# Row copies on two engines, second-head buffers and reordered tasks in a one-core hybrid decoder layer

## The chip, the cores and the metric

The kernel runs on one core of a Trainium2 chip. The metric is device time in microseconds (us) of one execution. The engines are named as in the profile: PE (TensorE, matrix multiply), PEld (its weight loads), DVE (VectorE), ACT (ScalarE), POOL (GpSimd) and SP (SyncE, which issues most of the DMAs). Each engine works through its own queue in order.

## The reference

One decoder layer for 256 tokens behind 16 learned meta tokens (272 rows in all), width 4096, in f32. A first projection (4096 to 16384 columns) gives eight kinds of columns, and two branches of 16 heads (or channel groups) of 128 use them:

```
h = rmsnorm(x, norm_g)
q, k, v, g_attn, b_conv, c_conv, h_conv, z_conv = split(h @ w_in)      # 8 x 2048 columns
# stick-breaking attention, per head, keys s before query t only
A[t, s] = sigmoid(z_ts) * prod_{s<j<t} (1 - sigmoid(z_tj)),  z = q.k / sqrt(128)
o = group_rmsnorm((A @ v) * silu(g_attn), attn_norm_g, 16)
# short gated convolution, width 3, per channel
y = group_rmsnorm(b_conv * short_conv(c_conv * h_conv, conv_w) * silu(z_conv), conv_norm_g, 16)
out = rmsnorm(x + concat(o, y) @ w_out, final_norm_g)[16:]
```

## The kernel before, in words

**Splits.** Every f32 weight tile (128x1024, 512 KB) is split into a rounded part `wh` (a copy on ACT, line 399) and a rest `wl` (a subtraction on DVE, line 395). The activations are split once in the same way. Each product is then three fp32r matmuls: high by low, high by high, low by high. A tile pair of `wh` and `wl` lives in a ring of six (`RING`), so the split of a tile waits until PE has finished the sixth one before it.

**Pieces.** The whole kernel is a list of 880 pieces, numbered 0 to 879, that PE works through in order. The input projection has eight groups; group g makes the columns of heads 2g and 2g+1 (in the code u = 0 and u = 1) and of the two channel groups beside them. A group has two kinds of pieces. A block piece `p` (24 matmuls, lines 424 to 426) does eight 128-row steps of one head's k, v, c or h block, transposed (128 features by 272 or 258 positions). The row pieces make q, g, b and z by rows: a plain pair A, B has 12 matmuls of 512 columns in each piece (lines 432 to 435), and a pair treated as two-by-two blocks with seven products has four pieces A, B, T, U of 6, 3, 6 and 6 matmuls, for which DVE forms the sums T and U (lines 409 to 414).

**Zones.** A group begins with its R zone: four times two block pieces (the last c and h blocks of the group before) and a plain pair. Then follows its S zone: twelve times A, B, T, U and two block pieces (the first six blocks of the group itself). After the last group a Z zone follows, and then the output projection as groups 8 to 11 of row pieces, with eight thin pieces `o` at the end. Where the text below names piece numbers, 417 to 432 is the R zone of group 5, in which the attention of group 4 is done, and 433 begins its S zone.

**What sets the order.** The order of every queue is written out by hand. At step i the program issues the matmuls of piece i, then the split of the piece five further on (line 985 to 987), then what the end of a block needs, and then the tasks that are due at i. `later(at, fn)` puts a task on the list; a `yield k` in it means: go on k pieces later. `plan_group` gives the due pieces of a group's attention, counted from its last S piece (`fin[g]`, here 416). For each of the two heads there are four tasks:

- `scores`: two matmuls z on PE; one piece later zm on DVE (lines 738 and 740) and Abs, Tanh and Ln on ACT (743 to 745)
- `weights`: four operations on DVE with two scans (751 to 755); one piece later four Exp on ACT (761 to 764)
- `trans`: a DVE transpose (770) within 32x32 blocks; one piece later `blocks`, 16 small copies on ACT (562) that move the blocks to their places, and two smaller ones on DVE (774, 775)
- `po`: ten matmul instructions on PE (779 to 783) that multiply the weights with v, and one piece later a product on DVE (787)

Between Tanh, Ln and Exp the ACT engine loads function tables, which the profile shows as instructions of their own. `v_block` has a task of the same shape: a transpose (579), then 16 copies (562) and four (585) on ACT.

**Buffers.** In the pool `wk` a tile with a tag waits for the last use of the tile that had the tag before. The scores of both heads use the tags zm and zl. Of the eight PSUM banks the R zone leaves three to the tasks, and the S zone one, which is also the bank of its block pieces. So the transposes `mix_t` of the group before (`mxh` and `mxc`, line 702), six and eight quads into an S zone, need that DVE has read the block that ended just before them (`c_block`, line 592, reads the block of c).

**Group sums of the output.** For groups 0 to 6 the normalised branch outputs go to DRAM and come back by the pieces `m`, whose split (lines 371 and 372) is followed by sums on POOL (305 to 308) for the seven-product pairs. `out_sums` (line 869) empties four PSUM banks after the last U piece of an output group. `load_res` (858) loads residual and gain, on SP's queue, into tiles of which one has the tag cb1 of the last group's rows.

Of the kernel before, what the change touches and what calls it, by code (L numbers as in the profile page):

```python
# [8 lines left out]
F32 = mybir.dt.float32  # L9
# [101 lines left out]
def kernel(ctx, tc, xt, xin, xm, par, fg, w1, w2, out):  # L111
# [48 lines left out]
    for g in range(GROUPS, GROUPS + 4):  # L160
        for at_, j in enumerate(OUT_ORDER if g > GROUPS else OUT_FIRST):
            for q in "ABTU" if seven(g, j) else "AB":
                pieces.append((q, g, j))
                if g == GROUPS and (at_, q) in ((2, "A"), (3, "A"), (9, "A")):
                    pieces.append(ms[{2: 4, 3: 5, 9: 6}[at_]])
        fin[g] = len(pieces) - 1
# [3 lines left out]
    real = [i for i, p in enumerate(pieces) if p[0] in "ABTUpo"]  # L170
    nth = {i: q for q, i in enumerate(real)}

# [380 lines left out]

    def blocks(dst, src, n):

        d = dst.rearrange("p (c x) -> p c x", c=n)
        s = src.rearrange("p (c x) -> p c x", c=n)
        for i in range(4):
            for j in range(4):
                o = d[32 * j:32 * j + 32, :, 32 * i:32 * i + 32]  # L560
                x = s[32 * i:32 * i + 32, :, 32 * j:32 * j + 32]
                A.copy(out=o, in_=x)  # L562

# [8 lines left out]
    def v_block(u, src, at_):  # L572
        vt = wk.tile([P, L + META], F32, tag="vt", name=f"vt{u}")
        G.memset(vt[:, L:L + META], 0.0)
        V.tensor_tensor(out=vt[:, :L], in0=src, in1=rstd, op=ALU.mult)

        def vtrans():
            y = wk.tile([P, 416], F32, tag="zs", name=f"yv{u}")
            V.transpose(out=y[:, :L + META], in_=vt[:, :L + META])
            yield 1  # L580
            vv = wk.tile([P, 2 * P], F32, tag=f"vv{u % 2}", name=f"vv{u}")
            blocks(vv, y[:, :2 * P], 2)
            v3 = wk.tile([META, P], F32, tag=f"v3{u % 2}", name=f"v3{u}")
            for i in range(4):
                A.copy(out=v3[:, 32 * i:32 * i + 32], in_=y[32 * i:32 * i + META, 2 * P:2 * P + 32])
            hd[u, "v"] = (vv, v3)

        later(at_, vtrans)
# [21 lines left out]
    def plain_block(u, b, e):  # L610
# [3 lines left out]
        elif b == 1:  # L614
            v_block(u, ps[:, :L], after(e, 2 if u % 2 == 0 else 3))
        elif b == 2:
            c_block(u, ps[:, META - 2:L])
        else:
            h_block(u, ps[:, META - 2:L], after(e, 1))
# [110 lines left out]
    def scores(g, u):  # L730
# [5 lines left out]
        yield 1  # L736
        zm = wk.tile([P, 448], F32, tag="zm", name=f"zm{g}_{u}")[:, :ZW]
        V.scalar_tensor_tensor(out=zm[:, :144], in0=z[:, :144], scalar=rq[:, 0:1], in1=zmask[:, P:],
                               op0=ALU.mult, op1=ALU.add)
        V.scalar_tensor_tensor(out=zm[:, 144:], in0=z[:, 144:ZW], scalar=rq[:, 1:2], in1=zmask,  # L740
                               op0=ALU.mult, op1=ALU.add)
        l = wk.tile([P, 448], F32, tag="zl", name=f"zl{g}_{u}")[:, :ZW]
        A.activation(out=l, in_=zm, func=AF.Abs)
# [4 lines left out]
    def weights(g, u):  # L748
# [8 lines left out]

        za = wk.tile([P, 448], F32, tag="zm", name=f"za{g}_{u}")
        G.memset(za[:, 3 * P:], 0.0)
# [7 lines left out]
    def trans(g, u):  # L767
        za = gr[g].pop(("za", u))
        y = wk.tile([P, 448], F32, tag="zl", name=f"ya{g}_{u}")
        V.transpose(out=y, in_=za)  # L770
        yield 1
        blocks(at[:, P:], y[:, :3 * P], 3)

# [45 lines left out]
    def plan_group(g):  # L819
# [4 lines left out]
        later(after(f, 1), q_t, g)  # L824
        for u, z in ((0, 5), (1, 10)):
            later(after(f, z), scores, g, u)
            later(after(f, z + 3), weights, g, u)
            later(after(f, z + 5), trans, g, u)
            later(after(f, z + 8), po, g, u)
        e = ends[2 * g + 1, 3]  # L830
        later(after(e, 4) if end else slot(g + 1, 2), conv_t, (2 * g, 2 * g + 1))
        later(after(e, 6) if end else after(slot(g + 1, 2), 2), conv_out, g)
        later(after(f, 20), squares, g, "h")
        later(after(f, 19) if end else slot(g + 1, 4), squares, g, "c")
        later(after(f, 21) if end else after(slot(g + 1, 4), 1), norm, g)
        later(after(f, 23) if end else slot(g + 1, 6), mix, g, "h")
        later(after(f, 24) if end else slot(g + 1, 8), mix, g, "c")

# [30 lines left out]
    def out_sums(g):  # L869
# [8 lines left out]
        V.tensor_tensor(out=r12, in0=p5, in1=r12, op=ALU.add)  # L878
        V.tensor_tensor(out=r22, in0=p5, in1=r22, op=ALU.add)
        V.tensor_tensor(out=r12, in0=r12, in1=s, op=ALU.subtract)  # L880
        V.tensor_tensor(out=s, in0=p7, in1=s, op=ALU.add)  # L881
        V.tensor_tensor(out=r21, in0=r21, in1=s, op=ALU.add)
        V.tensor_tensor(out=r22, in0=r22, in1=s, op=ALU.subtract)
# [79 lines left out]
    for i in range(1 - SPLITS, n):  # L963
# [34 lines left out]
        elif p[0] in "ABTUm":  # L998
            mm_in(i)
            while halved < until:  # L1000
                split(halved)
                halved += 1
            g = p[1]
            if p[0] == "B" and p[2] in (10, 6):
                load_res(2 * (g - GROUPS) + (p[2] == (6 if g > GROUPS else 10)))
            if p[0] == "U" and p[2] == OUT_SJ[-1]:
                out_sums(g)
            if i == fin[g]:
# [96 lines left out]
```

## Time and profile before

| | |
|---|---|
| median of 3 runs | 1907.0 us (1905.54 to 1907.43) |
| profiled execution | 1903.0 us |
| its span, first to last instruction | 1901.0 us |
| mean granted TensorE clock | 0.979 |
| PE busy | 1818.4 us (96%) |
| DVE, ACT, POOL busy | 1504.2, 1204.9, 146.7 us |
| input projection with its attention | to about 1519 us |
| one group of it | about 190 us |

The profiled execution is 2 us longer than its span, and the median of the runs 4 us longer than the profiled execution. The view of waits lists for an engine and line what released it, then total, count and longest. The timeline gives start, duration, engine, line, operation, output and inputs, and in brackets the idle time just before; several like instructions in a row are merged (x4). In the table of windows the columns are busy time with counts by engine, then the granted clock of PE, the share of the DMA engines and GB/s.

### The profile page before, as it was taken

The page shows a single profiled execution, that of the slowest core. Times are in us where ns is not written, and L with a number is a line of the kernel's source. Part 1 is how long each engine was busy: PE and PEld are TensorE (multiplying, and loading weights), DVE is VectorE, ACT ScalarE, POOL GpSimd, SP SyncE. Part 2 cuts the span into 40 slices and gives each one's busy share as a digit, 9 for nine tenths or more (in the row PEclk, how much of TensorE's full clock was granted, in tenths as well). Part 3 has the DMA queues.
Part 4 walks back from the last instruction along what each step waited for, and adds up shares of the span by engine and source line. Part 5 has one row for each costly group of instructions (what it writes and reads, how often), then busy time and mean ns, then how long its engine had stood idle before and what let it go on. Part 6 is the DMA issues. An engine that isn't in the chain of part 4 may idle for free. (4 is left out here: it accounts for less than half of the span.)

```text
span 1901.0 us, 29647 instructions
## 1 busy us (share of the span) xinstructions
PE 1818.4 (96%) x10998; PEld 1633.5 (86%) x10998; DVE 1504.2 (79%) x1858; ACT 1204.9 (63%) x2012; POOL 146.7 (8%) x192
## 2 busy tenths in 40 slices
PE   9999999999999999999999999999999979999997
PEld 7899788978897989798979897989798967788897
DVE  6765789678967896789778967897689768998986
ACT  6755765676567656665666566656665775555553
POOL 2031010001000100010101000100010131000000
PEclk9999999999999999999999999999899989999999
DMA  8966457645764576457645764576457654575664
GB/s 302 323 234 215 147 190 252 212 145 192 248 214 147 194 246 211 151 192 244 211 154 192 243 211 153 193 245 213 146 192 244 221 185 163 199 239 203 229 207 181
DMA packets 116064, 393.64 MB, mean 207 GB/s; under 512 B 13008, under 2 KB 18256, under 8 KB 115920
## 3 DMA queue, kind: packets, MB, share of 16 engines
q1 hardware_dynamic: 111888, 388.08, 61.0%
q10 hardware_dynamic: 4032, 3.67, 0.6%
q8 instruction: 86, 1.41, 0.3%
q14 instruction: 58, 0.48, 0.1%
HBM read 380.17 MB, written 11.53 MB: 206 GB/s over the span
## 5 line engine op out<-in xcount | busy, mean ns | idle before, releaser
L395 DVE TENSOR_TENSOR wl<-raw,wh 128x1024 fp32r<-128x1024 f32 (+3 forms) x756 | 848.5, 1143 | 304.2 <-ACT wh L399 294.6
L399 ACT CAST wh<-raw 128x1024 fp32r<-128x1024 f32 (+3 forms) x756 | 707.8, 974 | 333.9 <-DVE raw L414 87.8
L426 PE MATMUL mm<-xs,wl 128*128 128x258 f32 (+1 forms) x2048 | 582.6, 284 | 4.8 <-DVE wl L395 4.8
L424 PE MATMUL mm<-xs,wh 128*128 128x258 f32 (+1 forms) x2048 | 585.4, 286 | 0.0
L425 PE MATMUL mm<-xs,wh 128*128 128x258 f32 (+1 forms) x2048 | 582.2, 284 | 0.0
L424 PEld LDWEIGHTS mm<-xs,wh 128*128 128x128 f32 x2048 | 386.1, 189 | 6.8 <-DVE cq L787 1.2
L426 PEld LDWEIGHTS mm<-xs,wl 128*128 128x128 f32 x2048 | 386.0, 188 | 6.2 <-DVE wl L395 6.2
L425 PEld LDWEIGHTS mm<-xs,wh 128*128 128x128 f32 x2048 | 386.1, 189 | 4.1
L432 PE MATMUL P<-wh,xs 128*128 128x512 f32 x604 | 239.1, 396 | 3.8 <-DVE cc L597 2.3
L399 ACT CAST wh<-t 128x1024 fp32r<-128x1024 f32 (+1 forms) x108 | 112.4, 1041 | 201.4 <-DVE t L409 114.1
L435 PE MATMUL P<-wl,xs 128*128 128x512 f32 x604 | 237.2, 393 | 0.5 <-DVE wl L395 0.5
L434 PE MATMUL P<-wh,xs 128*128 128x512 f32 x604 | 236.3, 391 | 0.0
L432 PE MATMUL P<-wh,mixl 128*128 128x512 f32 (+1 forms) x392 | 150.0, 383 | 1.9 <-DVE os L881 1.9
L435 PE MATMUL P<-wl,mixh 128*128 128x512 f32 (+1 forms) x392 | 149.2, 381 | 2.7 <-DVE wl L395 2.7
L434 PE MATMUL P<-wh,mixh 128*128 128x512 f32 (+1 forms) x392 | 148.8, 380 | 0.0
L395 DVE TENSOR_TENSOR wl<-t,wh 128x1024 fp32r<-128x1024 f32 (+1 forms) x108 | 131.7, 1220 | 12.2 <-ACT wh L399 12.2
L435 PEld LDWEIGHTS P<-wl,xs 128*128 128x128 f32 x604 | 114.1, 189 | 28.3 <-DVE wl L395 4.1
L432 PEld LDWEIGHTS P<-wh,xs 128*128 128x128 f32 x604 | 114.4, 189 | 26.8 <-ACT za L764 5.1
L409 DVE TENSOR_TENSOR t<-raw,raw 128x1024 f32<-128x1024 f32 (+1 forms) x108 | 131.8, 1220 | 2.3 <-DMA raw<-w 2.3
L434 PEld LDWEIGHTS P<-wh,xs 128*128 128x128 f32 x604 | 114.3, 189 | 20.0
L435 PEld LDWEIGHTS P<-wl,mixh 128*128 128x128 f32 x392 | 74.5, 190 | 16.3 <-DVE wl L395 4.4
L432 PEld LDWEIGHTS P<-wh,mixl 128*128 128x128 f32 x392 | 74.7, 191 | 14.4 <-DVE os L881 2.4
(246 smaller groups left out, 2102.7 us busy)
## 6 DMA issues: line engine op xcount, KB each, us to landing
raw<-w SPq DMA_DIRECT2D x614, 512.0 KB, 4.3
lent<-sumd SPq DMA_DIRECT2D x49, 512.0 KB, 6.1
raw<-w SPq DMA_DIRECT2D x32, 384.0 KB, 3.8
raw<-xin SPq DMA_DIRECT2D x8, 512.0 KB, 5.7
xr<-xt SPq DMA_DIRECT2D x15, 272.0 KB, 5.6
sumd<-lent SPq DMA_DIRECT2D x7, 512.0 KB, 3.0
raw<-mixd SPq DMA_DIRECT2D x7, 512.0 KB, 4.9
res<-xin SPq DMA_DIRECT2D x12, 256.0 KB, 4.7
```

The costliest lines, as they stand in the source:

```text
L395: nc.vector.tensor_tensor(out=lo[:, c], in0=t[:, c], in1=h[:, c].bitcast(F32), op=ALU.subtract)
L399: nc.scalar.copy(out=h[:, c], in_=t[:, c])
L409: nc.vector.tensor_tensor(out=s[:, :2 * hw].rearrange("p (a b) -> p a b", a=2), in0=a[:, :2 * hw].rearrange("p (a b) -> p a b", a=2), in1= ...
L424: nc.tensor.matmul(out=o, lhsT=h, rhs=x[:, 0, s:], start=k == 0, stop=False)
L425: nc.tensor.matmul(out=o, lhsT=h, rhs=x[:, 1, s:], start=False, stop=False)
L426: nc.tensor.matmul(out=o, lhsT=lo, rhs=x[:, 0, s:], start=False, stop=k == KC - 1)
L432: nc.tensor.matmul(out=o, lhsT=a[1], rhs=h, start=key not in begun, stop=False)
L434: nc.tensor.matmul(out=o, lhsT=a[0], rhs=h, start=False, stop=False)
L435: nc.tensor.matmul(out=o, lhsT=a[0], rhs=lo, start=False, stop=last)
```

## The change

It has five parts.

1. `blocks` is cut into two halves of eight copies, the second one piece after the first, and of the eight copies four run on ACT and four on DVE. This holds for the attention weights (16 units, 32x96 elements a copy) and for v (16 units, 32x64).
2. The second head's scores and weights get their own buffers: two of the tag u2 in place of zm, and kT0 in place of zl.
3. The due pieces of a group's attention change. Before, the first head had 5, 8, 10, 13 (scores, weights, trans, po) and the second 10, 13, 15, 18. Now the first has 4, 7, 10, 13 and the second 6, 9, 13, 17. In the last group squares, norm and mix come one piece earlier (in the others only `squares` of the attention branch does). The v task of the first head starts six pieces after its block and not two.
4. The `m` pieces of groups 4, 5 and 6 stand later in output group 8: behind the fifth, sixth and eighth pair in place of the second, third and ninth (counted from 0).
5. In the output groups `out_sums` is issued ahead of the split of its step, and in it the second read of the product P5 comes after the read of P7.

```diff
-                if g == GROUPS and (at_, q) in ((2, "A"), (3, "A"), (9, "A")):
-                    pieces.append(ms[{2: 4, 3: 5, 9: 6}[at_]])
+                if g == GROUPS and (at_, q) in ((5, "A"), (6, "A"), (8, "A")):
+                    pieces.append(ms[{5: 4, 6: 5, 8: 6}[at_]])
...
-    nth = {i: q for q, i in enumerate(real)}
+    nth = {i: sum(k < i for k in real) for i in range(n)}
...
-    def blocks(dst, src, n):
+    def blocks(dst, src, n, half):
...
-        for i in range(4):
+        for i in (0, 1) if half == 0 else (2, 3):
             for j in range(4):
                 o = d[32 * j:32 * j + 32, :, 32 * i:32 * i + 32]
                 x = s[32 * i:32 * i + 32, :, 32 * j:32 * j + 32]
-                A.copy(out=o, in_=x)
+                if (i + j) % 2:
+                    V.tensor_copy(out=o, in_=x)
+                else:
+                    A.copy(out=o, in_=x)
...
-            blocks(vv, y[:, :2 * P], 2)
+            blocks(vv, y[:, :2 * P], 2, 0)
+            yield 1
+            blocks(vv, y[:, :2 * P], 2, 1)
...
-            v_block(u, ps[:, :L], after(e, 2 if u % 2 == 0 else 3))
+            v_block(u, ps[:, :L], after(e, 6 if u % 2 == 0 else 3))
...
-        zm = wk.tile([P, 448], F32, tag="zm", name=f"zm{g}_{u}")[:, :ZW]
+        zm = wk.tile([P, 512], F32, tag="u2", name=f"zm{g}_{u}", bufs=2) if u else wk.tile([P, 448], F32, tag="zm", name=f"zm{g}_{u}")
+        zm = zm[:, :ZW]
...
-        l = wk.tile([P, 448], F32, tag="zl", name=f"zl{g}_{u}")[:, :ZW]
+        l = wk.tile([P, 448], F32, tag="kT0" if u else "zl", name=f"zl{g}_{u}")[:, :ZW]
...
-        blocks(at[:, P:], y[:, :3 * P], 3)
+        blocks(at[:, P:], y[:, :3 * P], 3, 0)
+        yield 1
+        blocks(at[:, P:], y[:, :3 * P], 3, 1)
...
-        for u, z in ((0, 5), (1, 10)):
-            later(after(f, z), scores, g, u)
-            later(after(f, z + 3), weights, g, u)
-            later(after(f, z + 5), trans, g, u)
-            later(after(f, z + 8), po, g, u)
+        for u, at_ in enumerate(((4, 7, 10, 13), (6, 9, 13, 17))):
+            for k, fn in zip(at_, (scores, weights, trans, po)):
+                later(after(f, k), fn, g, u)
...
-        V.tensor_tensor(out=r22, in0=p5, in1=r22, op=ALU.add)
         V.tensor_tensor(out=r12, in0=r12, in1=s, op=ALU.subtract)
         V.tensor_tensor(out=s, in0=p7, in1=s, op=ALU.add)
+        V.tensor_tensor(out=r22, in0=p5, in1=r22, op=ALU.add)
...
             mm_in(i)
+            g = p[1]
+            if p[0] == "U" and p[2] == OUT_SJ[-1]:
+                out_sums(g)
             while halved < until:
                 split(halved)
                 halved += 1
```

The first place is ACT's queue in the R zone of group 5 (pieces 417 to 432), where the attention of group 4 is done. The names zm4_0 and zm4_1 are those of the first and the second head; wh428 is the split of piece 428. Before:

```order
L399 CAST wh428_9818<-raw428_9692 128x1024
L399 CAST wh429_9836<-raw429_9732 128x1024
L399 CAST wh430_9874<-raw430_9765 128x1024
L761 ACT_TABLE_LOAD
L761 ACTIVATE za4_0_9878<-zs4_0_9840 128x256
L762 ACTIVATE za4_0_9878<-zs4_0_9840 128x128
L763 ACTIVATE za4_0_9878<-zs4_0_9840 128x16
L764 ACTIVATE za4_0_9878<-zs4_0_9840 128x16
L399 CAST wh431_9910<-raw431_9804 128x1024
L399 CAST wh432_9931<-raw432_9822 128x1024
L562 COPY at_109<-ya4_0_9914 32x3x32 x16
```

And with the change, at the same place:

```order
L399 CAST wh428_9821<-raw428_9692 128x1024
L749 ACTIVATE zl4_1_9833<-zm4_1_9830 128x416
L750 ACT_TABLE_LOAD
L750 ACTIVATE zl4_1_9833<-zl4_1_9833 128x416
L751 ACT_TABLE_LOAD
L751 ACTIVATE zl4_1_9833<-zl4_1_9833,half_120 128x416
L399 CAST wh429_9851<-raw429_9722 128x1024
L768 ACT_TABLE_LOAD
L768 ACTIVATE za4_0_9855<-zs4_0_9825 128x256
```

The second head's Abs, Tanh and Ln, which stood behind the first head's copies, now stand ahead of the first head's Exp, with a table load ahead of Tanh that was not there; the second head's Exp in turn needs no load of its own.

The second place is DVE's queue in the same zone, from the last of the first head's four operations of `weights` to its transpose. Before:

```order
L755 TENSOR_TENSOR zs4_0_9840<-zm4_0_9797,zl4_0_9800 128x416
L395 TENSOR_TENSOR wl430_9875<-raw430_9765,wh430_9874 128x1024
L395 TENSOR_TENSOR wl431_9911<-raw431_9804,wh431_9910 128x1024
L770 STREAM_TRANSPOSE ya4_0_9914<-za4_0_9878 128x448
L395 TENSOR_TENSOR wl432_9932<-raw432_9822,wh432_9931 128x1024
L774 COPY at_109<-ya4_0_9914 16x16
```

And with the change:

```order
L761 TENSOR_TENSOR zs4_0_9825<-zm4_0_9752,zl4_0_9755 128x416
L744 SCALAR_TENSOR_TENSOR zm4_1_9830<-z4_1_9804,rq_124,zmask_113 128x144
L746 SCALAR_TENSOR_TENSOR zm4_1_9830<-z4_1_9804,rq_124,zmask_113 128x272
L395 TENSOR_TENSOR wl429_9852<-raw429_9722,wh429_9851 128x1024
L395 TENSOR_TENSOR wl430_9891<-raw430_9772,wh430_9890 128x1024
L757 SCALAR_TENSOR_TENSOR zs4_1_9894<-zm4_1_9830,zl4_1_9833 128x416
L759 SCALAR_TENSOR_TENSOR zl4_1_9833<-one_118,zs4_1_9894 128x144
L759 SCALAR_TENSOR_TENSOR zl4_1_9833<-one_118,zs4_1_9894 128x272
L761 TENSOR_TENSOR zs4_1_9894<-zm4_1_9830,zl4_1_9833 128x416
L395 TENSOR_TENSOR wl431_9926<-raw431_9807,wh431_9925 128x1024
L777 STREAM_TRANSPOSE ya4_0_9929<-za4_0_9855 128x448
```

Both the second head's zm and its four operations of `weights` moved ahead of the first head's transpose.

The third place is DVE's queue at the end of output group 8, where `out_sums` empties the banks (P4_8 is the product P1, P5_8 P5, P6_8 P7 and P7_8 P6). Before:

```order
L395 TENSOR_TENSOR wl742_16583<-raw742_16541,wh742_16582 128x1024
L876 TENSOR_TENSOR res0_15754<-P4_8_16247,res0_15754 128x512
L877 TENSOR_TENSOR os8_16586<-P7_8_16304,os8_16586 128x512
L878 TENSOR_TENSOR res0_15754<-P5_8_16287,res0_15754 128x512
L879 TENSOR_TENSOR res1_15755<-P5_8_16287,res1_15755 128x512
L880 TENSOR_TENSOR res0_15754<-res0_15754,os8_16586 128x512
L881 TENSOR_TENSOR os8_16586<-P6_8_16291,os8_16586 128x512
```

And with the change:

```order
L883 TENSOR_TENSOR res0_15770<-P4_8_16263,res0_15770 128x512
L884 TENSOR_TENSOR os8_16582<-P7_8_16310,os8_16582 128x512
L885 TENSOR_TENSOR res0_15770<-P5_8_16295,res0_15770 128x512
L886 TENSOR_TENSOR res0_15770<-res0_15770,os8_16582 128x512
L887 TENSOR_TENSOR os8_16582<-P6_8_16299,os8_16582 128x512
L888 TENSOR_TENSOR res1_15771<-P5_8_16295,res1_15771 128x512
L889 TENSOR_TENSOR res1_15771<-res1_15771,os8_16582 128x512
L890 TENSOR_TENSOR res1_15771<-res1_15771,os8_16582 128x512
L395 TENSOR_TENSOR wl742_16593<-raw742_16541,wh742_16592 128x1024
```

The split wl742 moved behind the eight operations, and the read of bank P6_8 stands one operation nearer to the front of them.

More of the change, by code (lines that the diff above doesn't have):

```diff
@@ L756, in weights @@
         yield 1
-        za = wk.tile([P, 448], F32, tag="zm", name=f"za{g}_{u}")
+        za = wk.tile([P, 512], F32, tag="u2", name=f"za{g}_{u}", bufs=2) if u else wk.tile([P, 448], F32, tag="zm", name=f"za{g}_{u}")
+        za = za[:, :448]
         G.memset(za[:, 3 * P:], 0.0)
@@ L768, in trans @@
         za = gr[g].pop(("za", u))
-        y = wk.tile([P, 448], F32, tag="zl", name=f"ya{g}_{u}")
+        y = wk.tile([P, 448], F32, tag="kT0" if u else "zl", name=f"ya{g}_{u}")
         V.transpose(out=y, in_=za)
         yield 1
-        blocks(at[:, P:], y[:, :3 * P], 3)
+        blocks(at[:, P:], y[:, :3 * P], 3, 0)
+        yield 1
+        blocks(at[:, P:], y[:, :3 * P], 3, 1)
         V.tensor_copy(out=at[:META, P - META:P], in_=y[96:96 + META, 400:416])
@@ L832, in plan_group @@
         later(after(e, 6) if end else after(slot(g + 1, 2), 2), conv_out, g)
[L833 to L837, printed above, removed]
+        later(after(f, 19), squares, g, "h")
+        later(after(f, 18) if end else slot(g + 1, 4), squares, g, "c")
+        later(after(f, 20) if end else after(slot(g + 1, 4), 1), norm, g)
+        later(after(f, 22) if end else slot(g + 1, 6), mix, g, "h")
+        later(after(f, 23) if end else slot(g + 1, 8), mix, g, "c")
     res, fgs, acc, sqs = [], {}, [], []
@@ L1002 @@
                 halved += 1
-            g = p[1]
             if p[0] == "B" and p[2] in (10, 6):
                 load_res(2 * (g - GROUPS) + (p[2] == (6 if g > GROUPS else 10)))
-            if p[0] == "U" and p[2] == OUT_SJ[-1]:
-                out_sums(g)
             if i == fin[g]:
```

## The prediction

> **What bounds the kernel now.** I read the page's busy shares first, then the waits of PE, then the timeline and the table of windows at the places of those waits.
>
> ```profile
> span 1901.0 us, 29647 instructions
> PE 1818.4 (96%) x10998; PEld 1633.5 (86%) x10998; DVE 1504.2 (79%) x1858; ACT 1204.9 (63%) x2012; POOL 146.7 (8%) x192
> ...
> PE po L779 <- ACT at L562: 39.3, 9, 7.4
> PE mxh L702 <- DVE cc L592: 11.5, 7, 1.7
> PE mm L426 <- DVE wl L395: 4.8, 7, 0.7
> PE P L432 <- DVE cc L597: 2.3, 7, 0.4
> ...
> 412.10:418.90 6.80, 6.80 (x19) 5.19 (x19) 6.73 (x8) 3.66 (x9) 0.00 (x0) 0.50 0.61 213
> ...
> 1560.96 0.80 PE L779 MATMUL po<-vv,at 128*128 128x128 f32 x2 [7.40 <-ACT at L562]
> ```
>
> PE bounds the span, so only its idle time and its slow time can be won. Of 82.6 us idle, 39.3 stand before `po`: 4.2 us in each of the seven R zones that follow groups 0 to 6, always at the second head, and the rest in the last group (7.40 there). The window row shows a second price: after such a wait PE runs at half clock for about 6.8 us, which loses 3.4. So a boundary costs 4.24 + 0.32 (the last wait row, 2.3 by 7) + 3.4 = 8.0 us, and seven cost 56.
>
> **The change part by part: the seven boundaries.** The question is when the first head's 16 copies are done now, since `po` of the first head stands at the same piece as before (after 429), and the second head's chain has moved ahead of it. These are rows of group 4's boundary.
>
> ```profile
> 936.47 0.28 PE L424 MATMUL mm<-xs,wh 128*128 128x258 f32 x1
> 963.11 0.38 PE L779 MATMUL po<-vv,at 128*128 128x128 f32 x2
> 964.50 0.39 PE L424 MATMUL mm<-xs,wh 128*128 128x258 f32 x1
> ...
> 938.79 0.90 ACT L585 COPY v<-yv 16x32 f32<-16x32 f32 x4
> 944.24 0.55 ACT L743 ACTIVATE zl<-zm 128x416 f32<-128x416 f32 x1 [2.53 <-DVE zm L740]
> 945.40 1.28 ACT L745 ACT_TABLE_LOAD   x1
> 946.69 0.64 ACT L745 ACTIVATE zl<-zl,half 128x416 f32<-128x416 f32 x1
> 947.24 2.94 ACT L399 CAST wh<-raw 128x1024 fp32r<-128x1024 f32 x3
> 952.94 0.42 ACT L761 ACTIVATE za<-zs 128x256 f32<-128x256 f32 x1 [1.46 <-DVE zs L755]
> 953.68 1.98 ACT L399 CAST wh<-raw 128x1024 fp32r<-128x1024 f32 x2
> 956.55 4.49 ACT L562 COPY at<-ya 32x96 f32<-32x96 f32 x16 [0.90 <-DVE ya L770]
> ...
> 943.72 0.49 DVE L740 SCALAR_TENSOR_TENSOR zm<-z,rq,zmask 128x272 f32<-128x272 f32 x1
> 950.58 0.58 DVE L751 SCALAR_TENSOR_TENSOR zs<-zm,zl 128x416 f32<-128x416 f32 x1
> 952.82 1.22 DVE L395 TENSOR_TENSOR wl<-raw,wh 128x1024 fp32r<-128x1024 f32 x1
> 955.88 0.64 DVE L770 STREAM_TRANSPOSE ya<-za 128x448 f32<-128x448 f32 x1
> 957.75 0.16 DVE L775 COPY a<-ya 16x16 f32<-16x16 f32 x1
> ```
>
> Steps read off them: Abs, Tanh, load, Ln take ACT 3.00 (944.24 to 947.24), and 4.28 with a second load of 1.28; four Exp 0.74; the four operations of `weights` 2.24 on DVE; zm 0.77; a split 1.05 on ACT (0.95 within a run) and 1.14 on DVE; a copy 0.28 on ACT. Before 936.47 the queues are as they were. With the change, in this group:
>
> - Piece 420 ends at 936.47 and frees the ring for 426: wh426 to 937.5, wl426 to 938.7, zm of the first head to 939.5.
> - ACT: its Abs to Ln 3.00, to 942.5; the second four v copies 1.0 and the four of line 585 0.9, to 944.4; wh427 to 945.5, wh428 to 946.4. Then ACT must wait.
> - DVE: wl427 behind wh427 to 946.6, the c block 0.34, wl428 to 948.1, `weights` of the first head 2.24 to 950.35, zm of the second to 951.1.
> - ACT: Abs to Ln of the second head, two loads, 4.28, to 955.4; wh429 to 956.5; load 1.3; the first head's Exp, 957.8 to 958.5; wh430 to 959.5 and wh431.
> - DVE: wl430 to 960.7; `weights` of the second head 2.24, to 962.9; wl431 to 964.1; only then the first head's transpose, to 964.7.
> - ACT: four copies to 965.9, wh433 to 966.9, four to 967.9. DVE: wl433 behind wh433 to 968.1, four copies, the two small ones: 969.0.
>
> PE wants `po` at 963.1 as before (two z products lie ahead of it in both), so **a wait of 5.9 us appears at the first head**. The price of a DVE copy of 32x96 isn't in the trace; the nearest rows:
>
> ```profile
> L774 DVE COPY at<-ya 16x16 f32<-16x16 f32 x16 | 2.7, 167 | 0.5
> L603 DVE TENSOR_SCALAR cy<-cc,pt 128x256 f32<-128x256 f32 x16 | 5.8, 364 | 0.6
> ```
>
> By elements 96 lies between them at about 0.23 us alone, and 0.15 in a run, since the two small copies start 0.09 apart. Only the last four of them lie on this chain (0.6; at the ends of the range 0.35 and 1.45), so the wait is 5.6 to 6.8.
>
> At the second head nothing waits: its transpose is done by 972.8, and after 969.0 `po` and pieces 430 to 433 take PE to about 983; the DVE queue (sums of pair 434, the h block, the convolution of 1.7) reaches its last copy at 981.6. That is 1.5 us of cover; if it is gone, each further us costs seven. The half clock remains: `po` doubles its 1.39 (963.11 to 964.50), and a block piece loses nearly half its speed for the remaining 4 us, 3.4 in all, as before. So a boundary costs 5.9 + 3.4 = 9.3 against 8.0: **+1.3 each, +9 for seven** (bounds +7 and +16; 0 if I am out by one split).
>
> On the clock, "TensorE: Matmul & The Clock Gate" (Part 1) of the Trainium skill says that PE drops to half rate after about 3.4 us without work and needs one busy window of 3.4 to come back. The waits of 4.24 agree with the first; the 6.8 us in the window row are two windows, not one, and I use the row.
>
> On table loads, the Trainium skill, "ScalarE: Activation LUTs" (What ACT_TABLE_LOAD costs), gives 1.28 us and a drain of 1.38 for each. Here Ln starts 0.01 after its load ends (945.40 + 1.28 to 946.69), so the trace shows no drain. With it the four loads on the chain would add 5.5, and the sum would end near 1950; the sum goes by the row.
>
> **S zones.** The v task of the first head moves from the second quad's start to the end of it, and half of its copies to DVE. The rows of group 5's S zone (the norm of the group before runs there too):
>
> ```profile
> 1030.48 4.06 ACT L562 COPY vv<-yv 32x64 f32<-32x64 f32 x16
> 1038.68 1.23 DVE L395 TENSOR_TENSOR wl<-raw,wh 128x1024 fp32r<-128x1024 f32 x1 [0.89 <-ACT wh L399]
> 1040.80 3.50 DVE L395 TENSOR_TENSOR wl<-raw,wh 128x1024 fp32r<-128x1024 f32 x3 [0.90 <-ACT wh L399]
> 1044.21 1.22 DVE L409 TENSOR_TENSOR t<-raw,raw 128x1024 f32<-128x1024 f32 x1
> 1050.96 0.42 DVE L592 TENSOR_TENSOR cc<-mm,rstd 128x258 f32<-128x258 f32 x1
> 1051.53 0.63 PE L702 MATMUL mxh<-ident,cq 128*128 128x128 f32 x4 [1.64 <-DVE cc L592]
> ```
>
> Today the 16 copies and four more hold ACT for 5 us, and DVE idles 1.75, 0.89 and 0.90 behind it. From 1044.21 DVE is full until the c block frees the bank. With the change the copies come behind wh468: wl467 ends at 1040.0, the transpose at 1040.4, ACT's first four at 1041.4, wl469 at 1043.6, and four DVE copies fill the time to 1044.2. So the sums start where they did, and PE restarts at 1051.5: the wait of 0.69 goes and returns in the next, 2.3 in one piece. Sum 0 (bounds -1 and +1 each). But one wait of 2.3 us may cost clock:
>
> ```profile
> 1588.20 0.47 PE L432 MATMUL P<-wh,osum 128*128 128x512 f32 x1 [2.32 <-DVE mixl L718]
> ...
> 1589.70:1593.10 3.40, 3.40 (x10) 2.62 (x9) 2.73 (x4) 2.10 (x4) 0.00 (x0) 0.50 0.71 292
> ...
> 1635.87 0.50 PE L432 MATMUL P<-wh,mixl 128*128 128x512 f32 x1 [1.95 <-DVE os L881]
> ```
>
> After 2.32 the clock halved for 3.4 us, a loss of 1.7; the waits of 1.64 and 1.95 cost none. If four of seven are hit that is 6.8, at most 12; I take **+4**.
>
> **The last group.** Here the splits of `m` pieces take places in the lead, and the same order hurts earlier.
>
> ```profile
> 1506.75 0.43 DVE L592 TENSOR_TENSOR cc<-mm,rstd 128x258 f32<-128x258 f32 x1 [2.95 <-PE mm L426]
> ...
> 1524.66 0.59 PE L432 MATMUL P<-wh,mixl 128*128 128x512 f32 x1
> ```
>
> From the c block's end, 1507.2, by the same steps: four DVE copies, wl690, one `m` rest and zm, to 1510.9; on ACT Abs to Ln, eight copies, one `m` copy and two splits, to 1518.7; on DVE the `m` rest, two splits, `weights` and the second zm, to 1523.3; ACT 4.3 for the second head, to 1527.6, and only then wh695, to 1528.7. PE wants piece 695 at 1524.66 as today, and waits 4. Exp, the second head's `weights`, the convolution and two splits lead to the first head's transpose at 1541.0 and its last copy at 1545.2, where PE has been waiting since 1540.5: `po` of the first head comes at 1545 and not 1536, and the second at 1561 as today, without the 7.40. To there the two are about even. Then it wins: the `m` sums are out of the way, and `mxc` comes at 1579 (six pieces of 12 matmuls at 0.23, and 1.8 for `po` and `mxh`, after 1560.8), not 1583.2. What hangs on that:
>
> ```profile
> 1583.86 0.33 SPq L866 DMA_DIRECT2D fg<-fg  x1
> 1590.30 1.22 DVE L409 TENSOR_TENSOR t<-raw,raw 128x1024 f32<-128x1024 f32 x1 [2.25 <-DMA raw<-w]
> ...
> 1866.75 0.39 PE L901 MATMUL mo<-keep,mixl 128*128 128x256 f32 x1 [1.88 <-DVE res L876]
> ```
>
> SP's queue stands at the gain's load, whose tile `mxc` has to leave, and the next weights wait behind it until 1590.30; from there to `out_sums` DVE has no gap. The DVE queue then starts about 4.2 us earlier and has two sums (1.2) less to do, and `out_sums` stands ahead of one split (1.2) with one operation (0.6) less before the bank that PE wants: together 7.2 us, of which PE can take nearly all: **-7** (bounds -12 and 0). At the end the 1.88 before `mo` go, since `out_sums` no longer stands behind splits that wait for weights: **-1.9**.
>
> **Sum.** 9 + 4 - 7 - 2 = +4 on 1903.0, the profiled execution (its span plus 2), so 1907; the median of the runs lies 4 above it, at 1907.0, and becomes **1911**.
>
> **The rivals.**
>
> - The clock doesn't care for 2.3 us. By the rule of the clock page of the Trainium skill named above, only windows without work count. The 1.95 without loss speaks for it, the 2.32 with loss against it. Then the +4 go: 1907, no change. Chance 0.27.
> - The boundaries are won: the first head's copies come by 963 and the second's too. All 56 us and 9 at the tail would go: 1842. If they come 4 us before my 969.0 the wait stays under 2, keeps the clock and wins 6 each: about 1860. It needs wl430 and `weights` of the second head not to stand ahead of the first head's transpose, and the order shows that they do. Chance 0.08.
> - The tail wins more, or the boundary is a split (1.1) shorter on ACT: 1897. The cover of 1.5 us at the second head speaks for nothing worse there. Chance 0.15.
> - Slower: DVE becomes the bound in the S zones. From 1044.21 to the c block it has no gap today; each us that the eight v copies and the transpose push it later is paid by PE before `mxh`, seven times, and past 2.3 us the clock falls each time. At 0.25 a copy started singly they take 1.0 us more than I put in: 7 more for the waits and 8 more for the clock, 1926. It decides from about 0.2 us a copy. Chance 0.15.
>
> **How the numbers follow.** My forecast has 0.35. A measurement here tells 0.2% (3.8 us) from no change. Faster by more: 0.23 (the two fast cases). Within: 0.29 (the clock rival and a little of the forecast). Slower: 0.48. The range of 8 in 10 is 1896 to 1926: it leaves out the won boundaries and the far slow end.
>
> **What would show it.** In the profile after: idle before `po` on the first head's instance, 5 to 7 us, seven times, and none on the second; half clock for about 7 us behind each; the wait before `mm` line 426 gone and the one before `mxh` near 2.3; weights line 409 before 1587; no idle before `mo`. Wrong would be a `po` without a wait in the R zones (the chain is shorter than I add up), a wait on both heads, or an S zone whose wait at `mxh` passes 3 us.

## The result and the profile after

The changed kernel takes **1939.2 us** (median of 4 runs, 1937.5 to 1940.0) against 1906.8 before: a ratio of 1.017, interval 1.0152 to 1.0187, 32 us slower. The forecast was 1911 in a range of 1896 to 1926: the sign was right, the size was not.

The page of the changed kernel and its table of PE's waits (total, count, longest):

```profile
span 1938.1 us, 29646 instructions
PE 1844.5 (95%) x10998; PEld 1653.0 (85%) x10998; DVE 1563.0 (81%) x2114; ACT 1147.1 (59%) x1756; POOL 136.6 (7%) x192
...
PE po L788 <- DVE at L563: 41.2, 7, 5.9
PE mxh L707 <- DVE cc L597: 21.7, 7, 3.1
PE P L432 <- ACT wh L399: 6.2, 2, 4.1
...
PE mo L908 <- DVE res L883: 0.8, 1, 0.8
```

The wait at `po` has moved to the first head and is 5.9 us, seven times, as forecast. `mm` line 426 no longer waits; `mxh` waits 3.1 and not 2.3. But PE was idle only 11.0 us longer than before (1938.1 - 1844.5 = 93.6, against 82.6), and PE's busy time grew by 26.1 with the same 10998 instructions. Part of that is half clock. The other part shows where nothing waits. These are the starts of pieces 493 (a P piece) and 505 (a block piece) in an S zone, before and after, with the clock granted in full:

```profile
1092.85 0.39 PE L432 MATMUL P<-wh,xs 128*128 128x512 f32 x1
...
1114.21 0.28 PE L424 MATMUL mm<-xs,wh 128*128 128x258 f32 x1
```

```profile
1123.12 0.40 PE L432 MATMUL P<-wh,xs 128*128 128x512 f32 x1
...
1144.90 0.28 PE L424 MATMUL mm<-xs,wh 128*128 128x258 f32 x1
```

The same twelve pieces, which the change doesn't touch, take 21.36 us before and 21.78 after. Over all undisturbed pieces of the trace (start to start) six matmuls of 512 columns take 1.39 us and not 1.36, 24 of 272 columns 3.01 and not 2.96. This is no wait and no clock, and the forecast had no term for it.

### The profile page after: what moved, and what is told of

It is laid out like the page before. It is cut to its first block, busy times and chain, and to the rows that moved or that the text cites. A ratio compares the mean times of both kernels' runs of the same rounds, so it can differ in the third digit from the quotient of the medians.

```text
span 1938.1 us, 29646 instructions
## 1 busy us (share of the span) xinstructions
PE 1844.5 (95%) x10998; PEld 1653.0 (85%) x10998; DVE 1563.0 (81%) x2114; ACT 1147.1 (59%) x1756; POOL 136.6 (7%) x192
## 4 chain that ended last, share of the span: by engine, by line
PE 81%; DVE 8%; ACT 7%; issue 3%; DMA 1%; POOL 0%; DVEq 0%; ACTq 0%; SPq 0%; POOLq 0%
PE P L432 14%; PE P L434 14%; PE P L435 14%; PE mm L424 11%; PE mm L425 11%; PE mm L426 11%; DVE wl L395 3%; ACT wh L399 2%; DVE zl L759 1%; DVE at L563 1%; ACT L751 1%; ACT zl L751 1%; ACT L768 1%; ACT L750 1%; PE po L792 0%
## 5 line engine op out<-in xcount | busy, mean ns | idle before, releaser
L399 ACT CAST wh<-raw 128x1024 fp32r<-128x1024 f32 (+3 forms) x756 | 715.2, 974 | 396.3 <-PE mm L425 169.8
L424 PE MATMUL mm<-xs,wh 128*128 128x258 f32 (+1 forms) x2048 | 592.2, 289 | 0.0
L426 PE MATMUL mm<-xs,wl 128*128 128x258 f32 (+1 forms) x2048 | 588.7, 287 | 0.0
L425 PE MATMUL mm<-xs,wh 128*128 128x258 f32 (+1 forms) x2048 | 588.6, 287 | 0.0
L424 PEld LDWEIGHTS mm<-xs,wh 128*128 128x128 f32 x2048 | 390.8, 191 | 6.2 <-issue 1.6
L425 PEld LDWEIGHTS mm<-xs,wh 128*128 128x128 f32 x2048 | 390.7, 191 | 4.7
L426 PEld LDWEIGHTS mm<-xs,wl 128*128 128x128 f32 x2048 | 390.2, 191 | 0.0
L432 PE MATMUL P<-wh,xs 128*128 128x512 f32 x604 | 241.8, 400 | 2.1 <-ACT wh L399 2.1
L434 PE MATMUL P<-wh,xs 128*128 128x512 f32 x604 | 239.8, 397 | 0.0
L409 DVE TENSOR_TENSOR t<-raw,raw 128x1024 f32<-128x1024 f32 (+1 forms) x108 | 132.2, 1224 | 0.4
```

The lines of the kernel that those rows point to most:

```text
L399: nc.scalar.copy(out=h[:, c], in_=t[:, c])
L409: nc.vector.tensor_tensor(out=s[:, :2 * hw].rearrange("p (a b) -> p a b", a=2), in0=a[:, :2 * hw].rearrange("p (a b) -> p a b", a=2), in1= ...
L424: nc.tensor.matmul(out=o, lhsT=h, rhs=x[:, 0, s:], start=k == 0, stop=False)
L425: nc.tensor.matmul(out=o, lhsT=h, rhs=x[:, 1, s:], start=False, stop=False)
L426: nc.tensor.matmul(out=o, lhsT=lo, rhs=x[:, 0, s:], start=False, stop=k == KC - 1)
L432: nc.tensor.matmul(out=o, lhsT=a[1], rhs=h, start=key not in begun, stop=False)
```

## Experiments on the place of the tiles

Part 2 of the change puts the second head's 448-wide tiles under the tag `kT0`, whose tile was 272 floats wide. The pool `wk` grows by 704 bytes, and the pool behind it, which holds `raw`, `wh` and `wl`, moves by as much. Addresses in the built programs, in bytes of a partition:

```
                 before    after
kT0 (wk)          27968    27968
first wh (wp)     59264    59968
first x tile     147264   147264
```

A pad stands in front of the ring (line 118, `pad_w`, 56 floats), so the ring can be moved alone. **The old order with the ring where the change puts it:**

```diff
-    wp.tile([P, 56], F32, name="pad_w", bufs=1)
+    wp.tile([P, 232], F32, name="pad_w", bufs=1)
```

> The kernel before, with one number changed: the pad in front of the weight ring is 232 floats instead of 56, so raw, wh, wl and all behind them in that stack lie 704 bytes further on, exactly where the change puts them (its second head's tile kT0 is 448 instead of 272 floats wide). No instruction is added, removed or moved. Place theory: the change lost most of its time because the operands of the matmuls lie elsewhere, so that six matmuls of a full P piece take 1.39 us and not 1.36 and 24 of a block piece 3.00 and not 2.96; in 688 undisturbed pieces that is 18.3 us, 23 over all 853, so this run takes 1928 to 1932 with no new wait. Rival, work beside PE: the pace fell because DVE does 256 copies more; then this run takes 1907 as before, with 1.36 and 2.96.

Measured: 1922.1 us, ratio 1.0079 (1.0058 to 1.01), with the waits of the kernel before at `po`, `mxh` and `mm` line 426 (39.2, 11.2 and 4.8 us in all). The same twelve pieces:

```profile
1107.79 0.40 PE L432 MATMUL P<-wh,xs 128*128 128x512 f32 x1
...
1129.57 0.28 PE L424 MATMUL mm<-xs,wh 128*128 128x258 f32 x1
```

21.78 us again, with not one instruction moved. The undisturbed pieces of this trace lose about 21 us, between the 18.3 and 23 that were expected; the median of the runs gives 15, less than expected. **The change with the ring 1024 bytes on** (pad 136 in place of 56, all else as in the change):

> The changed kernel with the pad in front of the weight ring 80 floats (320 bytes) wider, so that the ring lies 1024 bytes further on than before and not 704. Nothing else differs. Place theory (what counts is the address modulo 1024 or less): the pace is 1.36 and 2.96 again, and the run takes 1939 - 23 = 1916, within 1911 to 1919; what is left against 1907 is the price of the moved work itself. Rival, work beside PE: 1939, with 1.39 and 3.00.

Measured: 1919.3 us, ratio to the kernel before 1.0061 (1.0039 to 1.0083); the twelve pieces:

```profile
1111.65 0.39 PE L432 MATMUL P<-wh,xs 128*128 128x512 f32 x1
...
1133.01 0.28 PE L424 MATMUL mm<-xs,wh 128*128 128x258 f32 x1
```

21.36. So the place alone is worth 15 us in the old order and 20 in the new one, and the moved work 12. Five more kernels moved the ring of the kernel before, one of them the x tiles too (pad `pad_x` 40 to 56):

> The kernel before with the ring 256 bytes further on (pad 120 floats). Place theory: if 256 bytes is the period that counts, 1907 with 1.36 and 2.96; if it is longer, another time, 1907 to 1935. Rival: 1907.

> The kernel before with the ring 512 bytes further on (pad 184 floats). Place theory: if 512 bytes is the period that counts, 1907 with 1.36 and 2.96 and the run at 256 may differ; if it is longer, another time, 1907 to 1935. Rival: 1907.

> The kernel before with the ring 128 bytes further on (pad 88 floats). If the period of the address that counts is 128 bytes or less: 1907 with 1.36 us for six matmuls of a P piece and 2.96 for a block piece. If it is 256: slower, up to 1925, with another pace.

> The kernel before with the ring 64 bytes further on (pad 72 floats): the ring then lies 128 bytes past the x tiles modulo 256, where it was 64 before (1.36 us for six matmuls of a P piece, 2.96 for a block piece), 192 in the run at 128 (1.39, 3.04) and 0 in the run at 704 (1.39, 3.01). If only one of the four places is fast: 1.39 and about 3.0, 1922. If two are: 1.36 and 2.96, 1907. Faster than 1.36 would be a gain still open in the kernel before.

> The kernel before with the ring 704 bytes further on, as in the run that took 1922, and the x tiles (the other operand of the in-projection's matmuls) 64 bytes lower, so that the two lie to each other as before modulo 128. If it is the place of the two operands to each other that counts: 1.36 and 2.96 again, about 1907. If it is each operand's own place: 1.39 and 3.00 or worse stay, 1920 or more.

In the table, the distance is the address of the ring less that of the x tiles, modulo 256; pieces are medians of the undisturbed ones of the trace; a time marked * is of one execution.

| ring moved by | distance | six matmuls of P | 24 of a block (272 wide) | us |
|---|---|---|---|---|
| 0 (before) | 64 | 1.36 | 2.96 | 1906.9 |
| 256 | 64 | 1.36 | 2.96 | 1907.6* |
| 512 | 64 | 1.36 | 2.96 | 1905.2* |
| 704, x tiles -64 | 64 | 1.36 | 2.96 | 1912.6* |
| 64 | 128 | 1.37 | 3.04 | 1920.9* |
| 128 | 192 | 1.39 | 3.04 | 1924.3* |
| 704 | 0 | 1.39 | 3.01 | 1922.1 |

What counts is how the ring and the x tiles lie to each other, modulo 256 bytes: of four places tried one is fast, and the kernel before stood on it. The ring's own address doesn't decide: 704 bytes on it is slow with the x tiles in place and fast with the x tiles 64 bytes lower (one execution). The theory that DVE's added copies slow PE falls with the run at 704, which has none.

That each matmul's own two operands decide is not shown. For it: in the run with both moved, the P pieces of the output projection that read the group sums, whose tiles didn't move, stay at 1.39, while the pieces of 12 matmuls that read the mix tiles, which lie behind the ring and move with it, take 2.72 in every one of these runs. Against it: the T pieces of the S zones read no x tile, only group sums that lie behind the ring and move with it, and they take 1.36 in the kernel before, 1.39 with the ring 704 on, and 1.36 again when the x tiles alone are moved. The 1.39 is about 2 us of the 5.7 by which the run with both moved is slower than the kernel before, and the rest wasn't followed.

## Experiments on the moved work

All variants of the change below have the ring 1024 bytes on. First, where its 12 us lie. From the starts of the same pieces in two traces, against the trace before (stretches of 24 to 30 pieces around each zone):

| us against before | the change | change, ring right | old order, ring at 704 |
|---|---|---|---|
| seven R zones | +11.6 | +12.1 | +2.8 |
| seven S zones | +15.2 | +10.9 | +1.0 |
| last group and after, from piece 684 | -1.8 | -4.2 | +1.8 |
| the rest | +13.1 | +1.1 | +13.6 |

(Traces of the second column lie 2.5 above, that of before 4 below the median of its runs, so the sum of 20 there stands for the 12 of the medians.)

**S zones.** The v task goes back to what it was:

```diff
-                if (i + j) % 2:
+                if (i + j) % 2 and n == 3:
...
-            blocks(vv, y[:, :2 * P], 2, 0)
-            yield 1
+            blocks(vv, y[:, :2 * P], 2, 0)
             blocks(vv, y[:, :2 * P], 2, 1)
...
-            v_block(u, ps[:, :L], after(e, 6 if u % 2 == 0 else 3))
+            v_block(u, ps[:, :L], after(e, 2 if u % 2 == 0 else 3))
```

> The changed kernel with the ring 1024 bytes on, and the v copies as before: all 16 on ACT in one step, the first head's task due 2 pieces after its block and not 6. The copies of at and all else stay. S zone theory: the eight DVE copies (0.18 to 0.20 us each, 1.5) and the transpose now stand just ahead of the c block and push it by 1.0, and at 3.3 us of wait PE's clock is halved for 3.4 us each time; taken back, the wait before mm line 426 (0.7) comes back, the one before mxh falls to 1.6 to 1.7 with no half clock, and seven S zones cost 1.0 + 1.7 less each, at most 19: 1900 to 1907. In the R zones the four DVE and four ACT copies plus four of v3 that stand behind the first head's Ln are gone from there, which may shorten the first head's wait of 6.2 by up to 1. Rival, the halved clock doesn't come from the wait at mxh: then only the 7 of waits come back, 1912 to 1913.

Measured: 1913.6, ratio 1.0032 (1.0022 to 1.0042). Its waits:

```profile
PE po L787 <- DVE at L563: 51.7, 7, 7.4
PE mxh L706 <- DVE cc L596: 11.5, 7, 1.7
PE mm L426 <- DVE wl L395: 4.8, 7, 0.7
```

The S zone is as before, 1.65 and 0.7, and no clock is halved there. The wait at `po` grew by 1.2, where the expectation had it shrink: in the trace the second head's 20 v copies, 4.9 us on ACT, now all stand ahead of the first head's Abs (954.22) and PE comes to `po` 3.2 earlier against that Abs, while the chain behind it is only 2.05 shorter. By the starts of pieces, as in the table above, the S zones win 10.8 us and the R zones lose 5 (longer waits, but less half clock behind them: 7.0 us on average and not 8.0); the last group wins 3, and the medians of the runs show 5.7 in all. The time is near that of the rival, but its mechanism is not what happened: with waits of 1.65 in place of 3.3 no S zone has half clock any more.

How the S zone loses in the change, on DVE, group 5:

```profile
1067.88 0.47 DVE L582 STREAM_TRANSPOSE yv<-vt 128x288 f32<-128x288 f32 x1
1068.27 1.18 DVE L395 TENSOR_TENSOR wl<-raw,wh 128x1024 fp32r<-128x1024 f32 x1
1069.49 0.78 DVE L563 COPY vv<-yv 32x64 f32<-32x64 f32 x4
1070.50 1.23 DVE L395 TENSOR_TENSOR wl<-raw,wh 128x1024 fp32r<-128x1024 f32 x1 [0.23 <-ACT wh L399]
1071.76 0.79 DVE L563 COPY vv<-yv 32x64 f32<-32x64 f32 x4
1072.58 1.22 DVE L409 TENSOR_TENSOR t<-raw,raw 128x1024 f32<-128x1024 f32 x1
...
1079.90 1.09 PE L707 MATMUL mxh<-ident,cq 128*128 128x128 f32 x4 [3.09 <-DVE cc L597]
```

PE wants `mxh` at 1076.81. The sums of the pair (L409) begin 4.2 us ahead of that; before it was 5.7 (1044.21 against 1049.89). 1.45 us later on DVE, of which PE had 0.7 back at `mm`, is 0.76 more at `mxh`: 2.33 to 3.09.

**R zones.** The due pieces go back to those before; halves, pauses and own tiles stay:

```diff
-        for u, at_ in enumerate(((4, 7, 10, 13), (6, 9, 13, 17))):
+        for u, at_ in enumerate(((5, 8, 10, 13), (10, 13, 15, 18))):
```

> The changed kernel with the ring 1024 bytes on (1919 so far, with 6.2 us at the first head's po in each of seven boundaries), and the due pieces of scores, weights, transposes and po taken back to those before, (5, 8, 10, 13) and (10, 13, 15, 18); squares, norm and mix go back with them by one piece. The halved copies on two engines and the second head's own tiles stay. Order theory: the boundary is lost by the second head's Abs, Tanh and Ln standing ahead of the first head's Exp and its weights ahead of the first head's transpose; with the old pieces the first head waits for nothing, and at the second head the 4.5 us of copies on ACT become 2.3 twice on the way (they stood ahead of the second head's Abs, and they are its own last step), so the old wait of 4.2 shrinks to 0 to 1 and the half clock behind it goes: 6 to 8 less than before at each boundary, about 42 to 56 in all below the kernel before at the boundaries, against +4 to +14 now: 1855 to 1875. Rival, the copies themselves cost DVE too much (0.22 each, 16 per boundary, beside splits that PE waits for): the second head still waits about 4 us and the run takes 1905 or more.

Measured: 1928.7, ratio 1.0105 (1.009 to 1.012), slower than the change's own order. The order theory as stated there fell. Waits, then ACT in group 4:

```profile
PE po L788 <- ACT wh L399: 27.3, 8, 6.2
...
PE po L788 <- DVE at L563: 17.2, 7, 2.5
```

```profile
978.51 1.12 ACT L565 COPY at<-ya 32x96 f32<-32x96 f32 x4 [0.90 <-DVE ya L777]
981.34 0.55 ACT L749 ACTIVATE zl<-zm 128x416 f32<-128x416 f32 x1 [1.71 <-DVE zm L746]
981.92 0.55 ACT L750 ACTIVATE zl<-zl 128x416 f32<-128x416 f32 x1
982.49 1.28 ACT L751 ACT_TABLE_LOAD   x1
983.78 0.65 ACT L751 ACTIVATE zl<-zl,half 128x416 f32<-128x416 f32 x1
984.33 1.03 ACT L399 CAST wh<-raw 128x1024 fp32r<-128x1024 f32 x1
985.39 1.14 ACT L565 COPY at<-ya 32x96 f32<-32x96 f32 x4
```

The pause between the halves lets the second head's Abs, Tanh, table load and Ln in between: the first head's last four copies start 6.9 us after its first four. Now both heads wait (2.5 and 3.0), and in five of the seven groups both waits halve the clock. Against the kernel before, the R zones lose 15 us here and lost 12 with the change's own order. Most of the 9 us between the two orders lies in the S zones (20 against 11 us): the wait at `mxh` is the same, about 3.35, but it now halves the clock in all seven. Halving without the pause, as the only change to the kernel before:

```diff
-                A.copy(out=o, in_=x)
+                if (i + j) % 2 and n == 3:
+                    V.tensor_copy(out=o, in_=x)
+                else:
+                    A.copy(out=o, in_=x)
```

> The kernel before with one thing of the change alone: of the 16 copies of at, every second one goes to DVE, in one step as before (no pause between halves); all due pieces, tiles and addresses are those before. Halves theory: the first head's copies leave ACT 2.2 us earlier, but eight DVE copies of 0.22 stand ahead of the second head's zm, so its Abs starts only 0.6 earlier; its own DVE copies stand behind a convolution (1.7) and a split (1.2) and end near where ACT's ended: the second head's wait stays 3.5 to 4.2, and the run takes 1900 to 1908, no change. If halving alone is what the boundary needs, the wait falls under 2 and keeps the clock: 1850 to 1870.

Measured: 1908.1, ratio 1.0006 (0.9997 to 1.0016). No change, as expected; the wait per boundary, expected at 3.5 to 4.2, went from 4.2 to 4.6:

```profile
PE po L782 <- ACT wh L399: 31.9, 7, 4.6
```

Shorter copies were worth nothing here by themselves: what stands ahead of them on the queues decides.

**Tail.** Parts 4 and 5 alone, on the kernel before (the first two hunks and the last of the diff above, and the reordered operation in `out_sums`):

> The kernel before with the two tail parts of the change alone: the three m pieces two to three places later, and the output sums ahead of the splits with one operation put later. Row copies, tiles, due pieces and addresses as before. By the prediction's terms this is -7 and -1.9, 1898. From the trace of the change with the ring put right, where the pieces from 690 on win 4.2 against before and the wait at mo falls from 1.9 to 0.9: 1901 to 1904.

Measured: 1895.3, ratio 0.9942 (0.9927 to 0.9957): **11 us faster**, more than was expected. In the last group the waits at `po` fell from 2.3 and 7.4 to 1.3 and 2.5, the one before a P piece that needs `mixl` grew from 2.3 to 6.7, and the wait at `mo` fell to 0.7:

```profile
PE po L779 <- ACT at L562: 33.4, 9, 4.2
PE P L432 <- DVE mixl L718: 6.7, 1, 6.7
...
PE mo L901 <- DVE res L876: 0.7, 1, 0.7
```

In its trace the pieces from 684 on win 6.7; where the rest of the 11 lies, the traces don't show (that of before lies 4 below the median of its runs). In the change the row order takes part of it back in the last group, 4.2 in place of 6.7: the 4.1 before a P piece in the table after is piece 695, which the forecast had at 4.

## A version that beats both

If the queues decide, the order to try has the first head's Exp, transpose and copies ahead of the second head's Abs, without a pause, and the second head's copies ahead of the convolution:

```diff
-        for i in (0, 1) if half == 0 else (2, 3):
+        for i in range(4):
...
-                if (i + j) % 2:
+                if two and (i + j) % 2:
...
-            blocks(vv, y[:, :2 * P], 2, 0)
-            yield 1
-            blocks(vv, y[:, :2 * P], 2, 1)
+            blocks(vv, y[:, :2 * P], 2, u % 2)
...
-            v_block(u, ps[:, :L], after(e, 6 if u % 2 == 0 else 3))
+            v_block(u, ps[:, :L], after(e, 2 if u % 2 == 0 else 3))
...
-        blocks(at[:, P:], y[:, :3 * P], 3, 0)
-        yield 1
-        blocks(at[:, P:], y[:, :3 * P], 3, 1)
+        blocks(at[:, P:], y[:, :3 * P], 3, True)
...
-        for u, at_ in enumerate(((4, 7, 10, 13), (6, 9, 13, 17))):
+        for u, at_ in enumerate(((4, 7, 9, 13), (9, 11, 13, 18))):
```

> The changed kernel with the ring 1024 bytes on, the first head's v task as before (due 2, all on ACT), the second head's v copies and all at copies on two engines without the pause between halves, and due pieces (4, 7, 9, 13) and (9, 11, 13, 18), so that on each engine the first head's Exp, transpose and copies stand ahead of the second head's zm, Abs, Tanh and Ln, and the second head's copies ahead of the convolution. Order theory: no wait before either po in the R zones (first head's copies done about 3 us before its place, the second's 1 us before), no half clock there; the S zones as before (0.7 and 1.65); seven boundaries lose 0 to 1 each where they lost 8: 1850 to 1870. Rival, the engines have no room for it (DVE has 16 copies more at each boundary): waits of 2 us or more stay at po and the run takes 1890 or more.

Measured: 1880.7, ratio 0.9864 (0.9849 to 0.9878), between the two that were expected. No `po` waits in the R zones, but a new wait stands behind them. Waits, and DVE in group 4, where PE wants the bank of the second `po` at 972.52 for its next block:

```profile
PE mm L424 <- DVE cq L792: 30.3, 7, 4.3
```

```profile
969.78 3.49 DVE L395 TENSOR_TENSOR wl<-raw,wh 128x1024 fp32r<-128x1024 f32 x3
973.18 1.22 DVE L409 TENSOR_TENSOR t<-raw,raw 128x1024 f32<-128x1024 f32 x1
974.44 0.69 DVE L412 TENSOR_TENSOR raw<-raw,t 128x512 f32<-128x512 f32 x1
975.05 0.69 DVE L395 TENSOR_TENSOR wl<-raw,wh 128x512 fp32r<-128x512 f32 x1
975.77 0.69 DVE L414 TENSOR_TENSOR raw<-raw 128x512 f32<-128x512 f32 x1
976.38 0.42 DVE L792 TENSOR_TENSOR cq<-po,cq 128x256 f32<-128x256 f32 x1
```

The one product of 0.42 us that empties the bank (L792) stands behind three splits and the sums of a pair. Putting `po` of the second head one piece earlier (17 for 18), or two, moves it forward:

> The version that took 1881, with po of the second head due at piece 17 instead of 18; nothing else differs. Its output operation on VectorE then stands ahead of the sums of pair 440 and not behind them (4.9 us of VectorE work: three sums and two splits), just behind the split of 439. If the wait of 4.3 before the next block is only that operation's place: it would end at 973.6 on the scale of the run before where PE wants the bank at 972.5, a wait of 1.1 with no half clock: 7 times 3.2 and 1.7 less, 34, so 1845 to 1850. If VectorE has no room: the wait comes back at another place, and the run takes 1870 or more.

> The same with po of the second head due at piece 16. Its output operation stands one split further ahead (ends at 972.5, no wait there), but PE comes to po at 966.0 where the copies end at 966.8: a wait of 0.8 there. So 1842 to 1850, equal to the run at 17 within 4 us. If VectorE has no room: 1870 or more.

Measured: **1847 at 17** (ratio 0.9683, 0.9667 to 0.9699), as expected, and 1851.8 at 16 (0.9711), a little above what was expected: a wait of 6.3 at `po` in the last group, and waits of 1.3 to 2.0 before a P piece in four boundaries. At 17:

```profile
PE 1796.8 (97%) x10998; PEld 1618.6 (88%) x10998; DVE 1540.7 (83%) x2050; ACT 1155.1 (63%) x1820; POOL 144.5 (8%) x192
...
PE mxh L705 <- DVE cc L595: 11.5, 7, 1.7
...
PE mm L426 <- DVE wl L395: 4.8, 7, 0.7
PE mm L424 <- DVE cq L792: 4.4, 7, 0.6
...
PE po L784 <- ACT cb L632: 1.7, 7, 0.3
```

The seven boundaries lose 0.9 us each where they lost 8. DVE does 192 copies more than before and has room for them: 60 us faster than before, 92 faster than the change. By the starts of pieces in the traces, the R and S zones win 47 us of this, and the last group and the output projection, with parts 4 and 5, 8.5.

## Why the prediction was right and wrong

- **What was missing.** The failed step is in the change part by part: part 2, own tiles for the second head, was costed only as freedom for the order. That the wider `kT0` moves the ring was not asked, and the sum has no term for the pace of matmuls that nothing touches: it was put at nothing without a reason. The runs showed 15 us (old order) to 20 us (new order) for it, most of the miss of 28. All else together comes to 1919, in the range.
- **Boundaries.** The walk was right: 5.9 forecast, 5.88 measured, at the first head, seven times, none at the second. In the trace the second head's Abs to Ln (976.94 to 981.3) and its weights (986.51 to 988.8) stand ahead of the first head's transpose at 989.89, as added up:

```profile
976.94 0.55 ACT L749 ACTIVATE zl<-zm 128x416 f32<-128x416 f32 x1 [4.72 <-DVE zm L746]
986.51 0.59 DVE L757 SCALAR_TENSOR_TENSOR zs<-zm,zl 128x416 f32<-128x416 f32 x1
989.89 0.64 DVE L777 STREAM_TRANSPOSE ya<-za 128x448 f32<-128x448 f32 x1
995.13 0.55 PE L788 MATMUL po<-vv,at 128*128 128x128 f32 x1 [5.88 <-DVE at L563]
```

  That the two agree to 0.02 is luck: the copies took 0.3 more than was put in, and PE, slowed by the moved ring, came that much later; with the ring right the wait is 6.2. The size was +9; with the ring right it is +12, for this longer wait and for half clock that lasts 8.0 us behind it on average (7.2 to 8.8) where it was 7.0 before (5.6 to 8.6).
- **The DVE copy.** Taken at 0.15 in a run; measured 0.23 (L563, 32x96: 29.3 us in 128). Only 0.3 us of the chain hung on it.
- **S zones.** The term mis-sized. "The sums start where they did" was wrong: the walk had four DVE copies behind the last split and left out the four ahead of it, and the copies are 0.19 each. So 3.1 to 3.3 at `mxh` and not 2.3, which the forecast named as what would show it wrong; +11 with the ring right and +15 in the change, against +4. The rival "DVE becomes the bound in the S zones" (1926, 0.15) describes this better than the forecast.
- **Clock.** "Four of seven are hit" came out with the ring right; in the change all seven were. Half clock behind these waits lasts 22.7 us in the change and 15.8 with the ring right; at half speed that is 3.5 us more, most of the difference between 10.9 and 15.2. The rival that the clock doesn't care for 2.3 us is not borne out: in the run with the old due pieces it halved behind all seven waits of 2.46, and with `po` at 16 behind one of 2.01. But a wait of 2.37 in the last group of the change with the ring right kept the clock.
- **Tail and end.** -7 and -1.9 forecast; alone -11 in the medians, -6.7 and -1.1 in the trace; within the change with the ring right -4.2 and -1.0 (the wait at `mo` fell from 1.9 to 0.9).
- **Boundaries won** (0.08, 1842) is not what the change does, but the version above reaches 1847 by that mechanism, with another order.

## What to carry to other kernels

Before costing an edit that resizes a tile, write down the addresses of what lies behind it: here 704 bytes cost more than all the moved work (15 to 20 us against 12), without a wait to show it, only a pace of 1.39 for 1.36. Compare the start-to-start time of untouched pieces first; then look for waits. And moving small copies to a second engine paid here only when their places in both queues were moved too: look for the last operation that frees what PE wants next, and for what stands ahead of it.

## What the runs showed of the hardware

- The time of a matmul depends here on how the weight ring and the x tiles lie to each other modulo 256 bytes, 1.36 to 1.39 us for six of 512 columns and 2.96 to 3.04 for 24 of 272, at full clock; 24 of 258 columns changed by only 0.01 (2.87 before, 2.88 after). The Trainium skill, "SBUF — State Buffer" (SBUF: two separate sides), says that on the engines' side only the port pair of GpSimd and VectorE is contended for and that PE doesn't wait there. No wait shows here either, and yet the pace differs; whether this is a contention of PE's own two reads or something else, these runs don't show, and the T pieces above speak against a simple rule for each pair of operands.
- The half clock comes in steps of 3.4 us on a fixed grid, so the same wait may or may not be hit. In the change with the ring right its clock records show stretches of 3.41, 6.83 and 10.24 us at half clock, one, two and three steps of 3.413, and their starts lie whole steps apart (684.38 and 1070.08, for example, 113 steps). Behind waits at `mxh` of 3.34 (PE resumes at 491.28) and 3.33 (at 683.09):

```profile
491.30:494.70 3.40, 3.40 (x18) 2.92 (x19) 3.37 (x4) 1.49 (x4) 0.00 (x0) 1.00 0.85 254
684.40:687.70 3.30, 3.30 (x10) 2.53 (x9) 3.24 (x4) 1.52 (x2) 0.00 (x0) 0.50 0.64 220
```

  The first kept its clock, the second lost half of it (the column before the DMA share). Waits of 2.46 halved the clock too, and one of 2.01 in the run with `po` at 16; one of 2.37 did not, and those of 1.65 in the S zones never did.
